# Two buffers for a state space loop's tiles, a cached-row tile in the first stage's memory, and priority for the loop's body

## The chip, the cores and the metric

The kernel runs on one core of a Trainium2 chip. The metric is the time of one execution on the device in microseconds (us); lower is better. The engines are named as the profile names them: PE is TensorE (matmuls and transposes), PEld its weight loads, DVE is VectorE, ACT is ScalarE, POOL is GpSimd and SP is SyncE, which here only issues transfers (DMAs).

## What is computed

One inference step of one layer of a decoder, for a prompt of 512 tokens and for 8 sequences that are decoded one token further. The reference, cut to what matters here:

```python
mod = jnp.dot(jax.nn.silu(c), lp['w_ada']) + lp['b_ada']          # 6 x 1024 shifts, scales, gates
h = modulate(x, lp['norm_attn'], sh1, sc1)
u, q, k_c, v_c, k_s, v_s, k_w, v_w, g = jnp.split(jnp.dot(h, lp['w_in']), offsets, axis=-1)
o_ssm, s_last = ssm_mixer(u, ssm_s0, lp)      # 32 groups of 16 channels, 64 complex states each
o_attn, win_state = attend(q, gates, kv_cmp, kv_slc, kv_win)      # compressed, selected, window branch
x = x + gt1 * jnp.dot(jnp.concatenate([rmsnorm(o_ssm), rmsnorm(o_attn)]), lp['w_out'])
x = x + gt2 * jnp.dot(jnp.square(jax.nn.relu(jnp.dot(h2, lp['w_up']))), lp['w_down'])

def ssm_mixer(u, s0, lp):                     # per group: bu = u @ b_bar; s = lam_bar * s + bu; y = Re(s @ c)
    z = jax.nn.gelu(y + lp['ssm_d'] * u)
    return z * jax.nn.sigmoid(jnp.dot(z, lp['ssm_w_glu'])), s_last

def compress(kv, pe, w1, w2):                 # blocks of 32 cached rows become one row
    h = h_first[:, :-1] + h_second[:, 1:] + jnp.einsum('jd,jdh->h', pe, w1)
    return jnp.einsum('bngh,hd->bngd', jax.nn.gelu(h), w2)
```

`attend` for the 8 sequences compresses 1024 cached rows of each, gathered through a page table.

## The kernel before

The program is one function whose work a scheduler orders: it simulates the engines, and whenever an engine is free it takes the ready instruction that stands highest, which without a priority is the one written first. The order is fixed at build time; on the chip each engine takes its instructions in that order, waits included. Tiles come from pools. A tile with one buffer is written again only after its last reader of the round before; with two buffers, one round may be written while the other is read.

The work around the change, in program order:

- **Cached rows.** `load_cache(b)` gathers the rows of a sequence (POOL). `turned(bp)` transposes two sequences (a pair): 8 groups of four PE transposes `pxc` (L368), each into one of two buffers of the PSUM tag "tr", each taken to the tile `xc` by four copies; for the pairs 2 and 3 all four are ACT's (L375). `compressed(bp)` runs the matmuls `ph` (L387) on the two tiles `xc` of a pair. Of `xc` there are three buffers.
- **Modulation.** `ada(s, tag)` multiplies c by 512 columns of `w_ada`: eight matmuls `pada` (L334), whose weights `wada` (two halves of 1 MB) are loaded through SP's queue (L330) into a raw pool of three buffers; then ACT's copy `mrow` and four transposes `padt`.
- **Keys and values, queries.** `kv_proj` (matmuls `pkv`, L647); the query projection (matmuls `pj`, L605), whose PSUM buffers ACT empties with `ql` and `QS` (L912, L913).
- **The state space loop.** `for qd in range(8)` handles 4 of the 32 groups each, called a quad here. DVE builds the tables `BP` and `Cb` (L752 to L759); PE makes `pm` (L766) and `pbb` (L767); `M` goes to memory as `mscr` (L772) and comes back as the matrix `Tz` (L774), both through SP's queue; ACT copies `Bb` (L769). PE then multiplies the input `U` by `Bb` (`pvs`, L792), ACT copies the result as `Vs` and, with the complex halves turned, `Vp` (L230, L231); DVE forms `W`, scans it into `Rr` (L803), ACT turns that into `Rp`, DVE makes `Sx`, and PE adds `U`,`Tz` (L819) and `Sx`,`Cb` (L820) into `pys`. ACT copies `ys`, SP stores it as `yscr` (L822). The tiles are in the pool `sl`, one buffer each.
- Between quads stand `turned(2)` (ahead of quad 0), `compressed(2)` (quad 2), `turned(3)` (quad 3), `compressed(3)` (quad 5) and five `ada` (quads 1, 3, 4, 6, 7). `U` is loaded by eight transfers on SP's queue (L722) just ahead of quad 0.
- Afterwards `state_space_outputs` takes `yscr` back (`yc`), adds D times u (`yf`, L890) and applies the gelu (`zt`, L108 to L113), beside the query projection and the start of the attention, whose scores are `pst` (L1217) and whose exponentials are `pe` (L1227).

Of the kernel before, what the change touches and what calls it, by code (L numbers as in the profile page):

```python
# [9 lines left out]
F32 = mybir.dt.float32  # L10
# [6 lines left out]
P = 128  # L17
# [19 lines left out]
def body(tc, i, o, dbg=None):  # L37
# [174 lines left out]
    NG = 32  # L212
# [140 lines left out]
    def turned(bp):  # L353
        xc = [cp.tile([P, 2, 8, 132], F32, tag="xc", name="xc", bufs=3) for n in range(2)]
        for n in range(2):
# [229 lines left out]
    for k in range(KT):  # L585
        affine_split(p0, hH[:, k, 0:T], hL[:, k, 0:T], x_tile(k), bc[0], A1[:, k, 0:1], mod[:, k, 0:1])
    p0x.close()
    compressed(1, xcs.pop(1))

# [136 lines left out]
    yscr = dram.tile([NG // GQ, P, GQ, 80], F32, name="yscr")  # L726
    for qd in range(NG // GQ):

        if qd in (0, 3):
            b = 4 + 2 * (qd // 3)  # L730
            load_cache(b)
            load_cache(b + 1)
            xcs[b // 2] = turned(b // 2)
        if qd in (2, 5):
            compressed(2 + qd // 3, xcs.pop(2 + qd // 3))
        if qd in (1, 3, 4, 6, 7):
            ada((5, 6, 7, 8, 9)[(1, 3, 4, 6, 7).index(qd)], "ad")
        if qd == 6:
            compress_prompt()
            dump("Vbd", Vbd)  # L740
        gs = slice(qd * GQ, (qd + 1) * GQ)
# [8 lines left out]
        tmp = sl.tile(b4, F32, tag="tmp", name="tmp")  # L750
        BP = sl.tile(b4, F32, tag="BP", name="BP")
        nc.vector.tensor_tensor(BP, lam_b(lr, 0), vec_b(P1[:, gs]), ALU.mult)  # L752
# [22 lines left out]

        CT = sl.tile([P, GQ, 8, 8], F32, tag="CT", name="CT")
        ST = sl.tile([P, GQ, 8, 8], F32, tag="ST", name="ST")
        tq = sl.tile([P, GQ, 8, 8], F32, tag="tq", name="tq")
# [817 lines left out]
```

## Time and profile before

| | |
|---|---|
| Time, median of 3 runs | 898.34 us (898.29 to 901.24) |
| Profiled execution | 896.29 us, of which the span from first to last instruction is 894.6 us |
| PE busy | 844.3 us (94%), granted clock 0.992 on average |
| PEld, DVE, ACT, POOL busy | 747.3 (84%), 525.0 (59%), 388.2 (43%), 65.2 us (7%) |
| Chain that ended last | PE 86%, DMA 6%, ACT 3%, DVE 2%, issue 1% |

The profile is of one execution. Busy time is that of an engine's instructions; idle time stands in brackets before the instruction that ended it, with the releaser by the trace. The state space loop runs from about 128 to 259 us; the query projection and `state_space_outputs` from 259 to about 300.

### The profile page before, as it was taken

To read this page: it belongs to the slowest core of one execution; us is meant where nothing else is said; L and a number is where in the kernel's file an instruction comes from. 1 tells how busy PE (TensorE), PEld (TensorE's weight loads), DVE (VectorE), ACT (ScalarE), POOL (GpSimd) and SP (SyncE) were. 2 spreads that over 40 slices of the span, in tenths; PEclk is the share of its full clock that TensorE was granted. 3 is DMA by queue.
4 is the path that set the end of the run, shared out by engine and by line. 5 is a ranking of instruction groups with operands and counts; after the bars stand their busy time and mean duration, and the time that the engine had idled before them with its cause. 6 is when DMAs were issued, how large, how long until landed. Compare 5 with 4: busy or idle time off the path is not lost.

```text
span 894.6 us, 16415 instructions
## 1 busy us (share of the span) xinstructions
PE 844.3 (94%) x6517; PEld 747.3 (84%) x6517; DVE 525.0 (59%) x1413; ACT 388.2 (43%) x880; POOL 65.2 (7%) x147
## 2 busy tenths in 40 slices
PE   3799998999999899999889999999999999999995
PEld 2567897788998676756579999999999999999995
DVE  6676656759747975667578964443233444434534
ACT  2545326634435656546655554441111344433422
POOL 6001201000134200100000000000000000000000
PEclk9999999999999999999999999999999999999998
DMA  8956678366456620303257552333333333332202
GB/s 294 318 193 217 194 169 239 123 204 194 127 179 206 203 95 1 142 1 142 78 206 227 161 189 85 95 95 95 95 95 95 95 95 95 96 88 70 79 1 95
DMA packets 111836, 122.36 MB, mean 137 GB/s; under 512 B 24500, under 2 KB 91880, under 8 KB 109584
## 3 DMA queue, kind: packets, MB, share of 16 engines
q1 hardware_dynamic: 102256, 89.71, 33.0%
q0 software_dynamic: 5488, 29.99, 9.8%
q10 hardware_dynamic: 4016, 1.62, 0.7%
q8 instruction: 51, 0.84, 0.4%
q14 instruction: 25, 0.20, 0.1%
HBM read 112.47 MB, written 13.03 MB: 140 GB/s over the span
## 4 chain that ended last, share of the span: by engine, by line
PE 86%; DMA 6%; ACT 3%; DVE 2%; issue 1%; SPq 0%; ACTq 0%; DVEq 0%
PE pdn L1401 21%; PE pup L1401 20%; PE pj L605 5%; PE pwo L1401 5%; PE pkv L647 5%; PE ph L387 5%; DMA wada<-w_ada 5%; PE pada L334 2%; PE ptp L1246 2%; PE po L1253 2%; PE pS L1032 2%; PE pg L1273 2%; PE pst L1217 2%; PE pys L819 2%; PE pkT L1023 1%; PE pst L1218 1%
## 5 line engine op out<-in xcount | busy, mean ns | idle before, releaser
L1401 PE MATMUL pdn<-hidL,wH 128*128 128x256 f32 (+1 forms) x480 | 136.1, 284 | 0.0
L1401 PE MATMUL pdn<-hidH,wL 128*128 128x256 f32 (+1 forms) x480 | 135.9, 283 | 0.0
L1401 PE MATMUL pdn<-hidH,wH 128*128 128x256 f32 (+1 forms) x480 | 135.4, 282 | 0.0
L1401 PE MATMUL pup<-h2L,wH 128*128 128x256 f32 (+1 forms) x480 | 135.0, 282 | 0.0
L1401 PE MATMUL pup<-h2H,wL 128*128 128x256 f32 (+1 forms) x480 | 135.0, 282 | 0.0
L1401 PE MATMUL pup<-h2H,wH 128*128 128x256 f32 (+1 forms) x480 | 134.1, 283 | 0.0
L1401 PEld LDWEIGHTS pup<-h2L,wH 128*128 128x128 f32 x480 | 90.4, 188 | 0.8 <-DVE rs_t L97 0.8
L1401 PEld LDWEIGHTS pdn<-hidH,wL 128*128 128x128 f32 x480 | 90.6, 189 | 0.0
L1401 PEld LDWEIGHTS pdn<-hidL,wH 128*128 128x128 f32 x480 | 90.4, 188 | 0.1
L1401 PEld LDWEIGHTS pup<-h2H,wL 128*128 128x128 f32 x480 | 90.4, 188 | 0.0
L1401 PEld LDWEIGHTS pdn<-hidH,wH 128*128 128x128 f32 x480 | 90.4, 188 | 0.0
L1401 PEld LDWEIGHTS pup<-h2H,wH 128*128 128x128 f32 x480 | 89.6, 188 | 0.0
L63 ACT CAST wH<-wdn 128x1024 fp32r<-128x1024 f32 x30 | 31.5, 1050 | 114.0 <-PE pdn L1401 104.1
L64 DVE TENSOR_TENSOR wL<-wup,wH 128x1024 fp32r<-128x1024 f32 x30 | 36.7, 1224 | 58.1 <-ACT wH L63 58.1
L64 DVE TENSOR_TENSOR wL<-wdn,wH 128x1024 fp32r<-128x1024 f32 x30 | 36.8, 1225 | 54.2 <-ACT wH L63 54.2
L387 PE MATMUL ph<-xc,w 128*128 128x256 f32 (+2 forms) x320 | 65.4, 356 | 1.2 <-DVE xc L377 0.7
L387 PEld LDWEIGHTS ph<-xc,w 128*128 128x128 f32 x320 | 52.8, 203 | 12.9 <-issue 6.4
L63 ACT CAST wH<-wup 128x1024 fp32r<-128x1024 f32 x30 | 31.5, 1050 | 48.0 <-PE pup L1401 37.6
L1479 ACT ACTIVATE rl<-pup 128x256 f32<-128x256 f32 (+1 forms) x64 | 24.4, 384 | 48.9 <-PE pup L1401 48.8
L375 ACT COPY xc<-pxc 64x256 f32<-64x256 f32 x96 | 32.1, 366 | 20.8 <-DVE xc L377 18.2
L1410 DVE SCALAR_TENSOR_TENSOR xT<-pdn,mod,xT 128x256 f32<-128x256 f32 x32 | 15.2, 479 | 43.2 <-PE pdn L1401 43.2
L1480 DVE TENSOR_TENSOR rl<-rl 128x256 f32<-128x256 f32 (+1 forms) x64 | 27.1, 425 | 22.6 <-ACT rl L1479 22.6
(557 smaller groups left out, 2023.9 us busy)
## 6 DMA issues: line engine op xcount, KB each, us to landing
wada<-w_ada SPq DMA_DIRECT2D x20, 1024.0 KB
wup<-w_up SPq DMA_DIRECT2D x16, 1024.0 KB
wdn<-w_down SPq DMA_DIRECT2D x16, 1024.0 KB
wo<-w_out SPq DMA_DIRECT2D x8, 1024.0 KB
wada<-w_ada SPq DMA_DIRECT2D x8, 512.0 KB
rwin<-state_win SPq DMA_DIRECT2D x4, 1024.0 KB
new_win_sample<-state_win POOLq DMA_DIRECT2D x2, 2044.0 KB, 8.9
wkv<-w_in SPq DMA_DIRECT2D x3, 1024.0 KB
```

Of the source, the lines that this page charges most:

```text
L63: nc.scalar.copy(h, src)
L64: nc.vector.tensor_tensor(l, src, h, ALU.subtract)
L334: nc.tensor.matmul(ps[k % 4 * 32 : k % 4 * 32 + 32], cT[:, k], rs[k // kp][:, k % kp], start=(k < 4), stop=(k >= 4))
L375: nc.scalar.copy(dst[:, :, :, hf], srcv[:, :, :, hf])
L387: nc.tensor.matmul(phv[:, lo:hi, 0:w], w1[n][:, r_], xc[n][:, lo:hi, r_ % 8, off : off + w], start=(r_ == 0), stop=(r_ == 15))
L605: nc.tensor.matmul(ps[:, 0:HB], w[:, k], x[:, k, hc], start=(k == 0 and n == 0), stop=(k == KT - 1 and n == 2))
L647: nc.tensor.matmul(ps[0:mp, 0:nw], x[:, k, tok], w[:, k % 4], start=(k == 0 and n == 0), stop=(k == KT - 1 and n == 2))
L819: nc.tensor.matmul(py[:, c], Tz[:, :, :, g].rearrange("p t c -> p (t c)"), U[:, qd * GQ + g], start=True, stop=False)
L1032: nc.tensor.matmul(S[b4 * 32 : b4 * 32 + 32], q4[:, 4 * grp + b4], kts[b4], start=True, stop=True)
L1401: nc.tensor.matmul(ps[:, 0 : b - a], w, x[:, a:b], start=first and n == 0, stop=last and n == 2)
L1479: nc.scalar.activation(rl, ps[:, 0 : b - a], AF.Relu)
L1480: nc.vector.tensor_tensor(rl, rl, rl, ALU.mult)
```

## The change

It gives the tiles `BP`, `CT`, `ST`, `Vs`, `Vp` (shared with `Rp`), `W`, `W2`, `Rr` and `Sx` two buffers. `M`, `Bb`, `Cb`, `Tz`, `tmp`, `tq`, `rho` and `ys` keep theirs. `xc` gets two buffers instead of three; the first `xc` of pair 1 becomes a tile of the pool `p0`, the first stage's memory, and so `compressed(1)` is written ahead of that pool's end. The small tile `so` takes `tmp`'s memory. The quad's body becomes a function that is called under `tc.high_priority(300)`: the scheduler ranks its instructions higher than their place in the program would. No arithmetic is added or taken away.

```diff
     def turned(bp):
-        xc = [cp.tile([P, 2, 8, 132], F32, tag="xc", name="xc", bufs=3) for n in range(2)]
+
+        xc = [p0.tile([P, 2, 8, 132], F32, name="xc1") if (bp, n) == (1, 0) else cp.tile([P, 2, 8, 132], F32, tag="xc", name="xc", bufs=2)
+              for n in range(2)]
...
+    compressed(1, xcs.pop(1))
     p0x.close()
-    compressed(1, xcs.pop(1))
...
-    for qd in range(NG // GQ):
-
-        if qd in (0, 3):
...
+    def quad(qd):
         gs = slice(qd * GQ, (qd + 1) * GQ)
...
-        BP = sl.tile(b4, F32, tag="BP", name="BP")
+        BP = sl.tile(b4, F32, tag="BP", name="BP", bufs=2)
...
-        CT = sl.tile([P, GQ, 8, 8], F32, tag="CT", name="CT")
-        ST = sl.tile([P, GQ, 8, 8], F32, tag="ST", name="ST")
+        CT = sl.tile([P, GQ, 8, 8], F32, tag="CT", name="CT", bufs=2)
+        ST = sl.tile([P, GQ, 8, 8], F32, tag="ST", name="ST", bufs=2)
...
-        Vp = sl.tile([P, GQ, 64], F32, tag="Vp", name="Vp")
+        Vp = sl.tile([P, GQ, 64], F32, tag="Vp", name="Vp", bufs=2)
...
-        Sx = sl.tile([P, GQ, 81], F32, tag="Sx", name="Sx")
+        Sx = sl.tile([P, GQ, 81], F32, tag="Sx", name="Sx", bufs=2)
...
+    for qd in range(NG // GQ):
+
+        if qd in (0, 3):
+            b = 4 + 2 * (qd // 3)
+            load_cache(b)
+            load_cache(b + 1)
+            xcs[b // 2] = turned(b // 2)
+        if qd in (2, 5):
+            compressed(2 + qd // 3, xcs.pop(2 + qd // 3))
+        if qd in (1, 3, 4, 6, 7):
+            ada((5, 6, 7, 8, 9)[(1, 3, 4, 6, 7).index(qd)], "ad")
+        if qd == 6:
+            compress_prompt()
+            dump("Vbd", Vbd)
+        with tc.high_priority(300):
+            quad(qd)
```

(`Vs`, `W`, `W2`, `Rr` and `Rp` change as `Vp` does.) Each engine's instructions up to the end of the key and value projection keep their order but for a few table steps of DVE. Three places move; the line numbers of the changed kernel differ by 2 up to the loop, by 11 less inside it and by 6 more behind it.

PE at the end of `kv_proj(0)`, where the first quad meets pair 2. Before:

```order
L334 MATMUL pada<-wada,cT 32x512 x4
L368 MATMUL pxc<-ident,rc 128x128 x8
L792 MATMUL pvs<-U,Bb 128x72 x4
L368 MATMUL pxc<-ident,rc 128x128 x8
L334 MATMUL pada<-wada,cT 32x512 x4
L368 MATMUL pxc<-ident,rc 128x128 x4
L819 MATMUL pys<-U,Tz 128x80
L766 MATMUL pm_1644<-C_136,BP 128x16 x4
L368 MATMUL pxc<-ident,rc 128x128 x4
L339 MATMUL padt<-ident,mrow 128x128 x4
L767 MATMUL pbb<-ident,BP 128x128 x4
L387 MATMUL ph<-xc,w_155 128x2x128 x4
```

And with the change:

```order
L334 MATMUL pada<-wada,cT 32x512 x4
L781 MATMUL pvs<-U,Bb 128x72 x4
L370 MATMUL pxc<-ident,rc 128x128 x8
L808 MATMUL pys<-U,Tz 128x80
L755 MATMUL pm_1644<-C_136,BP 128x16 x4
L370 MATMUL pxc<-ident,rc 128x128 x4
L756 MATMUL pbb<-ident,BP 128x128 x4
L370 MATMUL pxc<-ident,rc 128x128 x4
L334 MATMUL pada<-wada,cT 32x512 x4
L370 MATMUL pxc<-ident,rc 128x128 x4
L781 MATMUL pvs<-U,Bb 128x72 x4
L809 MATMUL pys<-Sx,Cb 128x80
```

The first quad's `pvs` has moved ahead of all 32 transposes of the pair (12 stood ahead of it, four of them among the `pm` and `pbb` just before the rows shown); the second quad's `pvs` has moved ahead of the last 12. Six more `pys`, 12 transposes and the four `padt` then stand ahead of or among the first `ph`.

ACT at the same place. Before:

```order
L375 COPY xc<-pxc 64x4x64 x4
L769 COPY Bb<-pbb 128x512
L375 COPY xc<-pxc 64x4x64 x8
L793 COPY Vs<-pvs 128x288
L230 COPY Vp<-pvs 64x256
L231 ACTIVATE Vp<-pvs 64x256
L375 COPY xc<-pxc 64x4x64 x8
L230 COPY Rp<-Rr 64x256
L231 ACTIVATE Rp<-Rr 64x256
L336 COPY mrow<-pada 128x512
L375 COPY xc<-pxc 64x4x64 x8
L769 COPY Bb<-pbb 128x512
```

With the change, where the first `Bb` stands further up, among the copies `kvt`:

```order
L782 COPY Vs<-pvs 128x288
L230 COPY Vp<-pvs 64x256
L231 ACTIVATE Vp<-pvs 64x256
L377 COPY xc<-pxc 64x4x64 x8
L230 COPY Rp<-Rr 64x256
L231 ACTIVATE Rp<-Rr 64x256
L377 COPY xc<-pxc 64x4x64 x4
L758 COPY Bb<-pbb 128x512
L377 COPY xc<-pxc 64x4x64 x4
L336 COPY mrow<-pada 128x512
L377 COPY xc<-pxc 64x4x64 x4
L782 COPY Vs<-pvs 128x288
```

The 12 copies `xc` ahead of the first `Vs` are behind it now. Behind the rows shown come `Vp` twice, `ys` and nine copies `xc`. On SP's queue `wada`, which stood between `mscr` and `Tz` of quad 0, now stands behind that `Tz`.

ACT in the query projection, where `state_space_outputs` runs beside it. Before:

```order
L63 CAST wH<-wq 128x1024
L912 ACTIVATE ql<-pj 64x260
L913 ACTIVATE QS<-pj 64x252
L912 ACTIVATE ql<-pj 64x260
L913 ACTIVATE QS<-pj 64x252
L108 ACTIVATE zt<-yf 128x520
L111 ACTIVATE zt<-zt 128x520
L63 CAST wH<-wq 128x1024
L912 ACTIVATE ql<-pj 64x260
L913 ACTIVATE QS<-pj 64x260
```

With the change:

```order
L919 ACTIVATE QS<-pj 64x260
L63 CAST wH<-wq 128x1024
L111 ACTIVATE zt<-zt 128x520
L918 ACTIVATE ql<-pj 64x260
L919 ACTIVATE QS<-pj 64x252
L918 ACTIVATE ql<-pj 64x260
L919 ACTIVATE QS<-pj 64x252
L918 ACTIVATE ql<-pj 64x260
L919 ACTIVATE QS<-pj 64x260
```

The gelu's steps `zt` and the cast `wH` no longer both stand between two rounds of `QS`: the next cast `wH` comes after the `QS` that frees the PSUM buffer.

## Rows read from the trace of the kernel before

**Rows 1.** The page: busy time, share of the span and instructions of each engine; the chain that ended last, by engine.

```profile
PE 844.3 (94%) x6517; PEld 747.3 (84%) x6517; DVE 525.0 (59%) x1413; ACT 388.2 (43%) x880; POOL 65.2 (7%) x147
...
PE 86%; DMA 6%; ACT 3%; DVE 2%; issue 1%; SPq 0%; ACTq 0%; DVEq 0%
```

**Rows 2.** Busy time by stretch: the stretch and its length, then PE, PEld, DVE, ACT and POOL busy us (with instructions), the granted clock of PE, the DMA share and GB/s.

```profile
130.00:140.00 10.00, 8.54 (x76) 6.71 (x76) 7.11 (x23) 5.51 (x16) 0.00 (x0) 1.00 1.17 183
140.00:150.00 10.00, 8.93 (x60) 7.09 (x59) 6.67 (x19) 9.02 (x27) 2.99 (x5) 1.00 0.88 269
...
170.00:180.00 10.00, 8.82 (x62) 6.81 (x61) 8.25 (x21) 9.74 (x29) 0.89 (x3) 1.00 0.88 289
180.00:280.00 100.00, 99.94 (x747) 89.79 (x744) 69.86 (x182) 40.78 (x105) 20.21 (x49) 1.00 0.60 185
280.00:300.00 20.00, 18.66 (x123) 14.37 (x123) 16.33 (x38) 11.51 (x31) 8.11 (x21) 1.00 0.53 150
300.00:320.00 20.00, 16.75 (x104) 11.59 (x106) 16.57 (x63) 12.17 (x37) 1.48 (x6) 1.00 0.43 148
```

**Rows 3.** PE's timeline in the two stretches in which the loop meets a pair of cached rows: start, duration, line, operation, tiles, shape, count, and the idle time before it with its releaser. A matmul of the order above shows as two instructions here, a transpose as one.

```profile
134.96 1.07 PE L334 MATMUL pada<-wada,cT 128*32 128x512 f32 x8
135.96 1.09 PE L368 MATMUL pxc<-ident,rc 128*128 128x128 f32 x8
138.51 1.08 PE L792 MATMUL pvs<-U,Bb 128*128 128x72 f32 x8 [1.46 <-DMA new_cmp_sample<-kvs]
139.43 1.04 PE L368 MATMUL pxc<-ident,rc 128*128 128x128 f32 x8
141.53 1.07 PE L334 MATMUL pada<-wada,cT 128*32 128x512 f32 x8 [1.07 <-DMA wada<-w_ada]
...
143.45 1.00 PE L766 MATMUL pm<-C,BP 128*128 128x16 f32 x8
...
150.28 0.34 PE L820 MATMUL pys<-Sx,Cb 128*128 128x80 f32 x2
...
152.52 1.05 PE L792 MATMUL pvs<-U,Bb 128*128 128x72 f32 x8
...
173.86 1.06 PE L766 MATMUL pm<-C,BP 128*128 128x16 f32 x8 [0.55 <-ACT Vp L231]
...
178.23 1.99 PE L387 MATMUL ph<-xc,w 128*128 128x256 f32 x8 [0.52 <-ACT xc L375]
```

**Rows 4.** ACT's timeline in the first of these stretches, in the same columns.

```profile
134.73 1.29 ACT L375 COPY xc<-pxc 64x256 f32<-64x256 f32 x4 [0.88 <-PE pxc L368]
136.04 0.59 ACT L769 COPY Bb<-pbb 128x512 f32<-128x512 f32 x1
136.65 2.59 ACT L375 COPY xc<-pxc 64x256 f32<-64x256 f32 x8
139.63 0.40 ACT L793 COPY Vs<-pvs 128x288 f32<-128x288 f32 x1 [0.39 <-PE pvs L792]
...
140.43 0.38 ACT L231 ACTIVATE Vp<-pvs 64x256 f32<-64x256 f32 x1
...
143.74 0.41 ACT L231 ACTIVATE Rp<-Rr 64x256 f32<-64x256 f32 x1
...
152.72 0.43 ACT L821 COPY ys<-pys 128x320 f32<-128x320 f32 x1 [3.12 <-PE pys L820]
```

**Rows 5.** SP's queue: when transfers were issued and how long the issuing took; and behind it one piece of the chain that ended last (start, us, what), the time from issue to landing of `wada`.

```profile
127.00 5.11 SPq L722 DMA_DIRECT2D U<-uscr  x8
135.38 0.34 SPq L772 DMA_DIRECT2D mscr<-M  x1
...
138.62 0.37 SPq L774 DMA_DIRECT2D Tz<-mscr  x1
...
136.09 5.41 DMA wada<-w_ada
```

**Rows 6.** What DVE waited for between 125 and 260 us: engine, tile, line, releaser, then us in total, times and the longest.

```profile
DVE Cb L757 <- PE pys L820: 15.2, 5, 5.3
```

**Rows 7.** The query projection: PE's timeline, then ACT's.

```profile
281.34 0.39 PE L605 MATMUL pj<-hH,wH 128*128 128x260 f32 x1 [1.40 <-ACT QS L913]
...
278.12 0.64 ACT L111 ACTIVATE zt<-zt 128x520 f32<-128x520 f32 x1 [2.03 <-DVE zt L110]
278.88 1.04 ACT L63 CAST wH<-wq 128x1024 fp32r<-128x1024 f32 x1
...
280.92 0.37 ACT L913 ACTIVATE QS<-pj 64x260 fp32r<-64x260 f32 x1
```

**Rows 8.** The start of the attention: PE's timeline, then ACT's, then DVE's.

```profile
312.40 0.33 PE L1217 MATMUL pst<-KH,QS 128*128 128x128 f32 x1 [1.14 <-ACT pe L1227]
...
305.76 0.64 ACT L111 ACTIVATE zt<-zt 128x520 f32<-128x520 f32 x1
...
310.16 0.69 DVE L113 TENSOR_TENSOR uT<-zt,yf 128x520 f32<-128x520 f32 x1
```

**Rows 9.** Busy time by stretch, in the columns of rows 2, at places where PE stood idle for long.

```profile
14.00:18.00 4.00, 0.99 (x5) 0.62 (x4) 3.73 (x25) 1.47 (x4) 1.75 (x3) 1.00 1.07 312
...
36.00:40.00 4.00, 1.88 (x10) 0.85 (x10) 3.14 (x9) 2.71 (x9) 0.00 (x0) 1.00 1.02 392
40.00:44.00 4.00, 3.66 (x14) 2.00 (x15) 0.00 (x0) 0.00 (x0) 0.00 (x0) 0.57 1.04 386
```

More of the change, by code (lines that the diff above doesn't have):

```diff
@@ L726, in body @@
     yscr = dram.tile([NG // GQ, P, GQ, 80], F32, name="yscr")
-    for qd in range(NG // GQ):
-        if qd in (0, 3):
[L730 to L740, printed above, removed]
+    def quad(qd):
         gs = slice(qd * GQ, (qd + 1) * GQ)
@@ L786, in body @@
         nc.gpsimd.memset(rho[:, :, 0:1], 0.0)
-        Vs = sl.tile([P, GQ, 72], F32, tag="Vs", name="Vs")
+        Vs = sl.tile([P, GQ, 72], F32, tag="Vs", name="Vs", bufs=2)
         pvv = pst("ss", "pvs")
@@ L794, in body @@
         nc.vector.tensor_tensor(sn[:, :, gs], sn[:, :, gs], Vs[:, :, 64:72].rearrange("p g b -> p b g"), ALU.add)
-        Vp = sl.tile([P, GQ, 64], F32, tag="Vp", name="Vp")
+        Vp = sl.tile([P, GQ, 64], F32, tag="Vp", name="Vp", bufs=2)
         turn(Vp, pvv[:, 0 : GQ * 72].rearrange("p (g c) -> p g c", g=GQ)[:, :, 0:64])
-        W = sl.tile([P, GQ, 64], F32, tag="W", name="W")
-        W2 = sl.tile([P, GQ, 64], F32, tag="W2", name="W2")
+        W = sl.tile([P, GQ, 64], F32, tag="W", name="W", bufs=2)
+        W2 = sl.tile([P, GQ, 64], F32, tag="W2", name="W2", bufs=2)
         nc.vector.tensor_tensor(W, Vs[:, :, 0:64], CT, ALU.mult)
@@ L801, in body @@
         nc.vector.tensor_tensor(W, W, W2, ALU.add)
-        Rr = sl.tile([P, GQ, 64], F32, tag="Rr", name="Rr")
+        Rr = sl.tile([P, GQ, 64], F32, tag="Rr", name="Rr", bufs=2)
         nc.vector.tensor_tensor_scan(Rr.rearrange("p g c -> p (g c)"), rho.rearrange("p g c -> p (g c)"),
                                      W.rearrange("p g c -> p (g c)"), 0.0, ALU.mult, ALU.add)
-        Rp = sl.tile([P, GQ, 64], F32, tag="Vp", name="Rp")
+        Rp = sl.tile([P, GQ, 64], F32, tag="Vp", name="Rp", bufs=2)
         turn(Rp, Rr)
-        Sx = sl.tile([P, GQ, 81], F32, tag="Sx", name="Sx")
+        Sx = sl.tile([P, GQ, 81], F32, tag="Sx", name="Sx", bufs=2)
         nc.gpsimd.memset(Sx[:, :, 0:1], 0.0)
@@ L827, in body @@
     nc.tensor.transpose(px[0:NG, 256:384], SF, ident)
-    so = sl.tile([P, 384], F32, name="so")
+    so = sl.tile([P, 384], F32, tag="tmp", name="so")
     nc.vector.tensor_copy(so[:, 0:256], px[:, 0:256])
```

## Prediction

> **What bounds the kernel now.** I read the page first: PE is busy 94% of the span and holds 86% of the chain that ended last, ACT 3% and DVE 2% [rows 1]. No arithmetic changes, so the time can only move by PE's idle time, 894.6 - 844.3 = 50.3 us over the whole span. The second view is busy time by stretch, which says where that idle time lies. In the loop's first 50 us it is 1.46 us (130 to 140), 1.07 (140 to 150) and 1.18 (170 to 180), 3.71 together; from 180 to 280 us it is 0.06 us in 100 [rows 2]. So six of the eight quads already run beside a full PE. Right behind the loop it is 1.34 us (280 to 300) and 3.25 (300 to 320) [rows 2]. The rest lies at the start, from 320 us on and at the end, where the order changes little; I cost that at nothing, with about 1.5 us either way.
>
> The third view is PE's timeline at the two places, with the releaser of each wait [rows 3]. The first `pvs` waited 1.46 us for a transfer until 138.51. The transfer named is the tiny store of `kvs`; I take it for `U`, which `pvs` reads and whose last load was issued by 132.1 [rows 5]: nothing else that `pvs` needs is late, `Bb` being done at 136.63 [rows 4]. `pada` waited 1.07 us for `wada`, which took 5.41 us from issue to landing [rows 3, 5]. In the second place PE waited 0.55 and 0.52 us for ACT [rows 3], which was busy 9.74 of those 10 us [rows 2]: with all copies of a pair on it, ACT is the bound there. No wait repeats from quad to quad on PE. The one that does is DVE's: five times, 15.2 us together, `Cb` waits for the last `pys` of the quad before [rows 6]. That is the wait of a tile with one buffer, but `Cb` keeps one.
>
> One page of the notes bears on this. The Trainium skill, Perfetto Trace Analysis, section Optimization Strategy, says that a gap that keeps repeating on the engine that should be saturated can mean too few buffers. By that rule, read against the rows above, the second buffers are worth nothing on PE, at most the 0.06 us of 180 to 280; the repeating gap is on an engine that is not the bound, and its tile isn't doubled. By DVE's row alone one might hope for a share of 15.2 us.
>
> **Part by part.** *Buffers.* They remove waits of DVE, ACT and POOL, under a PE with 0.06 us idle: 0. That cover is gone only where PE waits already, at the two pairs and behind the loop, and there the order decides. *The tile `xc1` in the first stage's memory, and `so`.* PE's order up to the end of `kv_proj(0)` is as before; 0. *Priority.* It moves the quad's instructions past the transposes and copies of the pairs. I walked the new order with the durations of before.
>
> *First pair, PE.* Four transposes that stood ahead of `pada` take 0.5 us (eight took from 135.96 to 137.05); without them `pada` ends at about 135.5 instead of 135.96 [rows 3]. Behind it stands `pvs`, and `U` is there at 138.5: 3.0 us idle. Before, eight transposes (135.96 to 137.05) filled a part of it. Then:
> - `pvs` takes 0.9 us (138.51 to 139.43), eight transposes 1.0: 140.4. ACT, whose copies now can't start before `Vs`, does `Vs` and twice `Vp` until 140.8 [rows 4], then the first group of four copies, 1.29 us [rows 4], until 142.1. A `pys` and `pm` (0.1 and 1.0) end at 141.5, and the third group of transposes waits for a PSUM buffer: 0.6 us idle.
> - The third group and `pbb` (0.5 each) end at 143.1; the second group's copies at 143.4: 0.3 idle. The fourth group and `pada` (1.0) end at 144.9.
> - ACT does `Rp` twice (0.8), then the third group until 145.5: 0.6 idle before the fifth group. `Bb` of quad 1 (0.59) ends at 146.1, the fifth group at 146.0: 0.1 idle, then `pvs` until 147.0.
> - Seven `pys` (2.0, eight took from 150.28 to 152.52 [rows 3]), the sixth group, `padt` and the seventh (0.5 each) end at 150.5. ACT after `Bb`: the fourth group 147.4, `mrow` 148.0, the fifth group 149.3, `Vs`, twice `Vp` and `ys` 150.9, and `ph` needs three copies of the sixth group (in the row of 178.23 it started at the third copy's end), 151.9: 1.4 idle.
>
> Sum 3.0 + 0.6 + 0.3 + 0.6 + 0.1 + 1.4 = 6.0 us, where before it was 2.53 (1.46 + 1.07): **+3.5**. In it `wada`'s wait is 0: it now stands behind `Tz`, which was issued at 138.62; with 5.41 us it lands at 144.0 [rows 5], as `pada` is reached. The reason for the loss in one line: ACT did 12 copies, 3.9 us (1.29 + 2.59), while the first `pvs` waited for `U` [rows 4]. Now it waits too, and does them later.
>
> *Second pair.* The same walk with the quads 2 and 3, where no transfer is late, gives waits of 0.4, 0.8 and 0.3 = 1.5 us for 1.18: **+0.3**. Its bounds are 0 idle (-1.2), if the quads' earlier chains give ACT a lead, and 6.0 idle (+4.8), as in the first pair.
>
> *The query projection.* `pj` waited 1.40 us for `QS` [rows 7]. Ahead of those copies ACT had waited 2.03 us for DVE in the gelu, then did `zt` and the cast `wH` [rows 7]. In the new order `QS` of the next half stands ahead of the cast. Gain between 0 (another DVE wait in front of `QS`) and 1.4; I take **-1.0**, nearer the full one, since the cast's 1.04 us alone comes off the path.
>
> *Start of the attention.* The last quad's `pys` come some 6.7 us of PE's work earlier in the order, so the four rounds of `yf` and `zt` do too, by about 4 us; ACT's `zt` (0.64) and DVE's last step at 310.16 no longer stand between the softmax steps that PE waited for (1.14 us on `pe`) [rows 8]. Of the 3.25 us idle in 300 to 320 [rows 2] the gelu's instructions on ACT and DVE are about half of what was ahead of the waits; bounds 0 and -3.25, taken **-1.5**.
>
> Sum: 3.5 + 0.3 - 1.0 - 1.5 = +1.3 us. Against the profiled execution, 896.29, that is 897.6; the median of the runs is 2.05 higher, 898.34, which makes 899.6.
>
> **Rivals.** A measurement of this kernel can tell about 0.5%, 4.5 us: faster means below 893.85, slower above 902.83.
> - *Faster: the earlier quads win everywhere.* The first pair costs only `U` (+1.5) and saves `wada` (-1.07), because ACT catches up under `ph`; the second pair's 1.18, the 1.40 of `pj` and the 3.25 go: 898.34 + 0.4 - 5.8 = 892.9. For it: DVE's and ACT's chains do start earlier in the order. Against: PE has no other ready work at the first pair, as `ph` needs the very copies. Chance 0.2.
> - *Slower: ACT's queue bounds both pairs.* If the second pair costs what the first does (6.0 idle), the time is 899.6 + 4.5 = 904.1. ACT had 0.26 us to spare in 170 to 180 [rows 2], and each quad puts seven of its own copies, 3.0 us, ahead of the pair's. It decides from 4.7 us idle at the second pair on. Chance 0.2.
> - *The clock falls.* After 36 to 40 us, with PE busy 1.88 of 4 us, the granted clock was 0.57 for 4 us, which costs 4 x 0.43 = 1.7 us; after the 3.01 us of waiting in 14 to 18 us it stayed at 1.00 [rows 9]. If the idle time at 135.5 brings it down: 901.3. The Trainium skill, TensorE: Matmul & The Clock Gate, section Why this matters for your kernels, advises against long idle gaps between bursts of matmuls, which speaks for this rival; by that rule, too, it would be about 901. The rows show both outcomes. Chance 0.1.
> - *Nothing moves.* Loss and gains are hidden, the idle time at both pairs stays 3.7 us: 898.3. For it: 0.06 us in 100. Against: the first `pvs` has nothing to stand behind. Chance 0.1.
>
> **How the numbers follow.** The forecast itself has 0.4, within 896 to 903 by the bounds of its four terms taken singly. The time is 899.6. The range goes from the faster rival's 892.9 to the slower one's 904.1, with 0.6 of spread at either end: 892.5 to 904.7. Faster by over 0.5%: the faster rival less its upper edge, 0.18; slower: the slower rival and a little of the clock's, 0.22; the same 0.6.
>
> **What would show it.** Right: before the first `pvs` a wait of 3 us, and PE waiting at `pxc` and `ph` for ACT's copies between 140 and 153; no wait of `pada` for `wada`; the loop's idle time 7 to 8 us; less than 0.7 at `pj`; less than 2.5 in the 20 us after the projection. Wrong: a `pvs` that starts well before 138, which would say that not `U` was late; an ACT that is idle in the second pair; or a change of more than 2 us behind 320 us, which I set to nothing.

## The result, and the profile after

The change made the kernel slower: 908.93 us median of four executions (904.89 to 911.93), where the kernel before, run beside it, took 898.32 (895.51 to 901.24). The ratio is 1.0129, with a 95% interval of 1.0082 to 1.0175. The forecast was 899.6, in a range up to 904.7. The profiled execution of the change took 911.73 us, its span is 910.0 us, and the mean granted clock in it 0.985 (0.992 before).

The page of the profiled execution, busy time of each engine and the chain that ended last, to be held against [rows 1]:

```profile
PE 853.8 (94%) x6517; PEld 752.3 (83%) x6517; DVE 527.1 (58%) x1413; ACT 389.0 (43%) x880; POOL 64.6 (7%) x147
...
PE 80%; DMA 9%; DVE 5%; ACT 3%; issue 1%; SPq 0%; POOL 0%; DVEq 0%; ACTq 0%
```

The first thing to see is PE's busy time: 853.8 us where it was 844.3, with the same 6517 matmuls. 9.5 of the 15.4 us by which the span grew are not waits at all. So the ground of the prediction, that time can only move by PE's idle time, is gone before any wait is read.

Two things make the same matmuls longer: a lower clock, and an order in which they go less well together. To part them we used landmarks. The same matmuls lie ahead of the first `pj` (a projection ahead of the loop), the last `pj`, the last `po` that reads `PT` (the end of the attention), the first `pup` and the last `pup` in both kernels. So their start times can be subtracted. From each difference we take the time that the low clock cost: half of every stretch at the lower of PE's two levels, 1.2 instead of 2.4 GHz. What remains is waits and longer work. (In a stretch in which PE also waits, half of it is too much.)

| start of | before | after | difference | low clock | rest | rest since the landmark above |
|---|---|---|---|---|---|---|
| first `pj` | 93.1 | 93.6 | +0.5 | 0 | +0.5 | +0.5 |
| last `pj` | 295.2 | 305.6 | +10.4 | 5.1 | +5.3 | +4.8 (the loop) |
| last `po` | 448.9 | 459.9 | +11.1 | 5.1 | +6.0 | +0.7 (attention) |
| first `pup` | 503.5 | 515.9 | +12.5 | 5.1 | +7.4 | +1.4 (out-projection) |
| last `pup` | 786.6 | 802.1 | +15.4 | 6.8 | +8.6 | +1.3 (MLP) |

Of the 15.4 us the clock holds 6.8, the loop 4.8, the passage from the out-projection to the MLP 2.7, the rest 1.2. The loop's 4.8 can be parted once more: between its landmarks PE's idle time grew by 2.2 us (7.3 for 5.1) and its busy time by 7.7, of which the clock holds 5.1. So 2.2 us are waits and 2.6 us are longer work.

**The first pair.** Busy time by stretch, in the columns of [rows 2]; the third and fourth lines cut out the idle time and what came behind it:

```profile
130.00:140.00 10.00, 6.88 (x60) 5.16 (x59) 7.44 (x26) 1.22 (x3) 0.00 (x0) 0.97 1.00 111
140.00:150.00 10.00, 8.53 (x59) 6.96 (x58) 6.39 (x17) 8.73 (x25) 2.68 (x5) 0.86 0.68 210
136.00:139.00 3.00, 0.09 (x4) 0.00 (x0) 1.66 (x10) 0.00 (x0) 0.00 (x0) 1.00 0.89 104
139.00:143.00 4.00, 3.79 (x20) 3.83 (x21) 1.30 (x4) 1.93 (x6) 0.00 (x0) 0.57 0.75 206
```

PE's timeline there, as [rows 3], then ACT's, as [rows 4]:

```profile
135.03 1.06 PE L334 MATMUL pada<-wada,cT 128*32 128x512 f32 x8
139.21 1.71 PE L781 MATMUL pvs<-U,Bb 128*128 128x72 f32 x8 [3.12 <-DMA new_cmp_sample<-kvs]
140.70 1.92 PE L370 MATMUL pxc<-ident,rc 128*128 128x128 f32 x8
...
146.48 1.07 PE L334 MATMUL pada<-wada,cT 128*32 128x512 f32 x8 [0.97 <-DMA wada<-w_ada]
...
149.48 0.45 PE L809 MATMUL pys<-Sx,Cb 128*128 128x80 f32 x2 [0.50 <-POOL Sx L802]
...
153.54 1.99 PE L389 MATMUL ph<-xc,w 128*128 128x256 f32 x8 [0.24 <-ACT xc L377]
```

```profile
141.00 0.40 ACT L782 COPY Vs<-pvs 128x288 f32<-128x288 f32 x1 [5.73 <-PE pvs L781]
```

And `wada` in the chain that ended last, from issue to landing, as in [rows 5]:

```profile
139.46 6.98 DMA wada<-w_ada
```

This is the walk of the prediction: `pada` first, then nothing for `pvs` to stand behind, 3.12 us of waiting, and an ACT that does nothing for 5.73 us. The waits of the stretch are 3.12 + 0.97 + 0.50 + 0.24 = 4.83 us for 2.53 before. Behind the idle 3 us the clock fell to 0.57 of full in the four microseconds from 139, which costs 4 x 0.43 = 1.7 us.

**Inside the quads.** PE's timeline behind the second pair, of the change and then of before:

```profile
178.29 0.66 PE L370 MATMUL pxc<-ident,rc 128*128 128x128 f32 x4 [0.41 <-ACT xc L377]
179.60 0.66 PE L370 MATMUL pxc<-ident,rc 128*128 128x128 f32 x4 [0.66 <-ACT xc L377]
...
183.32 1.05 PE L334 MATMUL pada<-wada,cT 128*32 128x512 f32 x2
184.29 0.66 PE L400 MATMUL pk<-w2v,hg 128*128 128x64 f32 x4
...
185.33 1.06 PE L334 MATMUL pada<-wada,cT 128*32 128x512 f32 x6
186.32 0.66 PE L370 MATMUL pxc<-ident,rc 128*128 128x128 f32 x4
...
197.82 1.06 PE L334 MATMUL pada<-wada,cT 128*32 128x512 f32 x6
198.81 1.11 PE L781 MATMUL pvs<-U,Bb 128*128 128x72 f32 x8
199.85 1.91 PE L334 MATMUL pada<-wada,cT 128*32 128x512 f32 x10
201.68 0.48 PE L389 MATMUL ph<-xc,w 128*128 128x256 f32 x1
```

```profile
186.80 1.92 PE L334 MATMUL pada<-wada,cT 128*32 128x512 f32 x16
188.65 0.70 PE L387 MATMUL ph<-xc,w 128*128 128x256 f32 x2
```

The first two lines are the second pair's waits: 1.07 us, as before (0.55 + 0.52 [rows 3]). The `pada` lines are what nobody had looked for. A `pada` matmul writes 32 of the 128 output partitions, four of them stand in the order one behind the other, and PE runs the four side by side: eight instructions of the trace (four matmuls) take 1.00 us (135.03 to the next start, [rows 3] has the same), sixteen take 1.85 (186.80 to 188.65). Now the priority draws a quad's matmuls forward, through the middle of such a set. Two instructions alone then take 0.97 us (183.32 to 184.29), the six that were cut off from them 0.99 (185.33 to 186.32): nearly two full prices for one set. In the same way six and ten, cut by a `pvs`, take 0.99 + 1.83 where sixteen whole ones take 1.85. The order has three such cuts, each some 0.97 us dearer: **2.9 us of PE work** that the kernel before doesn't have. The same price shows, with the other sign, in the matmuls `psc` of the attention, which have the same shape (128x32): between the first and the last `pj` the change has them in one piece fewer, and they take 1.0 us less.

**Between out-projection and MLP.** PE's timeline, of the change and then of before; `bc` is the broadcast of the MLP norm's statistics, from which `h2H` and `h2L`, the operands of `pup`, are made:

```profile
513.11 0.29 PE L1407 MATMUL pwo<-mixH,wqL 128*128 128x264 f32 x1
513.23 0.61 PE L1378 MATMUL bc<-dg,ones 128*128 128x128 f32 x4
515.94 0.50 PE L1407 MATMUL pup<-h2H,wH 128*128 128x256 f32 x2 [2.10 <-ACT h2H L200]
...
517.40 0.39 PE L1407 MATMUL pup<-h2L,wH 128*128 128x256 f32 x1 [0.72 <-DVE h2L L201]
```

```profile
499.86 0.38 PE L1372 MATMUL bc<-dg,ones 128*128 128x128 f32 x2
...
503.35 0.29 PE L1401 MATMUL pwo<-mixH,wqL 128*128 128x264 f32 x1
503.47 0.40 PE L1401 MATMUL pup<-h2H,wH 128*128 128x256 f32 x2
```

Before, `bc` stood ahead of the last 26 `pwo`, and the norm's 2 to 3 us on ACT and DVE ran beside them; `pup` began without a wait. Now `bc` is PE's last instruction before `pup`, and the norm has nothing beside it: 2.10 + 0.72 us. This lies some 250 us behind the last quad.

**The clock.** Busy time by stretch at the two places, besides 139 to 143, where it was low in this profile and not in that of before:

```profile
224.00:232.00 8.00, 8.00 (x38) 5.30 (x37) 5.57 (x16) 3.24 (x6) 0.37 (x2) 0.57 0.05 8
...
514.00:518.00 4.00, 1.34 (x9) 1.14 (x10) 4.00 (x11) 1.69 (x4) 0.00 (x0) 1.00 0.24 85
518.00:522.00 4.00, 4.00 (x28) 3.98 (x30) 3.89 (x10) 2.39 (x5) 0.00 (x0) 0.57 0.81 265
```

The fall at 518 stands behind the idle time at `pup`. That at 224 doesn't: PE was busy 8.00 of 8 us. Three places, 4 + 8 + 4 us at 0.57, make 1.7 + 3.4 + 1.7 = 6.8 us. This profile lost more than the others: in the runs of experiment e4, by each execution's span and mean clock, four executions of the change lost 11.3 us to the clock on average and seven of before 8.3, a difference of 3.0; without it 894.1 us stand against 886.7, **+7.4**.

**The rest of the loop and the attention**, in the columns of [rows 2], and the query projection as in [rows 7]:

```profile
170.00:180.00 10.00, 8.94 (x64) 6.71 (x63) 6.91 (x20) 6.53 (x20) 1.04 (x4) 1.00 0.29 95
180.00:280.00 100.00, 99.17 (x683) 84.97 (x682) 61.14 (x165) 40.32 (x107) 14.58 (x42) 0.97 0.58 183
290.00:310.00 20.00, 19.01 (x137) 15.48 (x135) 15.79 (x36) 11.79 (x29) 7.99 (x21) 1.00 0.44 114
310.00:330.00 20.00, 17.49 (x88) 10.69 (x88) 16.95 (x64) 11.35 (x34) 1.68 (x6) 1.00 0.52 183
...
295.82 0.39 PE L607 MATMUL pj<-hH,wH 128*128 128x260 f32 x1 [0.58 <-ACT QS L919]
```

PE is still full from 180 to 280 (99.17 of 100), so the second buffers have nothing to give there, but the same work is longer. `pj` waits 0.58 for 1.40. In the 20 us around the start of the attention PE is idle 2.51 us for 3.25, yet by the landmarks the attention as a whole gained nothing (+0.7): over all of it PE waits only 0.1 us less, and its matmuls `pS`, again four side by side, stand in one piece more and take 1.1 us longer.

### The profile page after: what moved, and what is told of

Its sections match the earlier page's. It is cut to its first block, busy times and chain, and to the rows that moved or that the text cites. A ratio compares the mean times of both kernels' runs of the same rounds, so it can differ in the third digit from the quotient of the medians.

```text
span 910.0 us, 16408 instructions
## 1 busy us (share of the span) xinstructions
PE 853.8 (94%) x6517; PEld 752.3 (83%) x6517; DVE 527.1 (58%) x1413; ACT 389.0 (43%) x880; POOL 64.6 (7%) x147
## 4 chain that ended last, share of the span: by engine, by line
PE 80%; DMA 9%; DVE 5%; ACT 3%; issue 1%; SPq 0%; POOL 0%; DVEq 0%; ACTq 0%
PE pup L1407 20%; PE pdn L1407 20%; PE pwo L1407 5%; DMA wada<-w_ada 5%; PE ph L389 4%; PE pkv L649 3%; PE pada L334 3%; PE pj L607 3%; PE ptp L1252 2%; PE po L1259 2%; PE pg L1279 2%; PE pS L1038 2%; PE pys L808 1%; DMA yc<-yscr 1%; PE pst L1223 1%
## 5 line engine op out<-in xcount | busy, mean ns | idle before, releaser
L334 PE MATMUL pada<-wada,cT 128*32 128x512 f32 x192 | 34.2, 635 | 6.0 <-DMA wada<-w_ada 5.3
```

The costliest lines, as they stand in the source:

```text
L334: nc.tensor.matmul(ps[k % 4 * 32 : k % 4 * 32 + 32], cT[:, k], rs[k // kp][:, k % kp], start=(k < 4), stop=(k >= 4))
```

## Experiments

Each run is compared with the kernel before on the same chip. The table has what the edits below came to: the ratio with its interval; the rest against before, stretch by stretch, as in the table of landmarks; what the low clock cost in the loop and in the attention; the `pada` sets that are cut in the loop, and how much longer `pada` takes there; how many `pwo` stand behind `bc`; how many of PE's 1039 instructions in the attention stand elsewhere than before, by matching the orders of the two traces; and the whole rest once more, over all executions.

| run | median | ratio | rest: loop, attention, out-proj., MLP | clock: loop, att. | cuts, `pada` | `pwo` behind `bc` | moved in att. | rest, all executions |
|---|---|---|---|---|---|---|---|---|
| the change | 908.93 | 1.0129 [1.0082, 1.0175] | +4.8 +0.7 +1.4 +1.3 | 5.1, 0 | 3, +2.9 | 0 | 102 | as e4 |
| e4, again | 907.33 | 1.0126 [1.0100, 1.0152] | +3.3 +0.4 +1.4 +1.4 | 3.4, 0 | 3, +3.0 | 0 | 102 | +7.4 |
| e1 | 918.30 | 1.0236 [1.0182, 1.0290] | -2.5 +3.4 +2.5 +0.9 | 1.7, 17.1 | 0, 0 | 0 | 602 | +8.9 |
| e2 | 912.59 | 1.0171 [1.0121, 1.0221] | -4.0 +4.0 +0.9 0 | 3.4, 10.2 | 1, +1.0 | 26 | 663 | +3.5 |
| e3 | 905.65 | 1.0109 [1.0081, 1.0137] | +4.1 -0.5 0 0 | 5.1, 1.7 | 3, +2.8 | 26 | 87 | +5.4 |
| e5 | 903.82 | 1.0064 [1.0034, 1.0095] | +0.2 0 +2.3 +1.4 | 3.4, 0 | 0, 0 | 0 | 92 | +3.7 |
| e6 | 905.50 | 1.0092 [1.0063, 1.0122] | +5.5 -0.2 0 0 | 6.8, 1.7 | 4, +3.9 | 26 | 87 | +6.1 |
| e7 | 909.91 | 1.0125 [1.0085, 1.0165] | +5.6 -0.1 +1.7 +1.1 | 5.1, 0 | 5, +4.8 | 0 | 87 | +8.5 |
| e8 | 910.83 | 1.0131 [1.0088, 1.0174] | +5.6 -0.1 +2.3 +1.4 | 3.4, 1.7 | 3, +2.9 | 0 | 95 | +8.6 |
| e9 | 899.98 | 1.0027 [0.9994, 1.0060] | +0.1 -0.2 0 0 | 6.8, 1.7 | 0, +0.1 | 26 | 92 | +2.6 |
| e10 | 907.54 | 1.0107 [1.0082, 1.0131] | +0.4 -0.9 +2.3 +1.2 | 0, 6.8 | 0, 0 | 0 | 653 | +3.8 |
| e11 | 903.99 | 1.0069 [1.0028, 1.0111] | +2.9 -0.7 +1.7 +0.5 | 1.7, 1.7 | 0, +0.2 | 0 | 87 | +4.7 |

The rest and the clock stretch by stretch come from one profiled execution each, so single entries scatter by a microsecond or more (e4 is the change once more, and its loop shows +3.3 for +4.8); what lies ahead of the first `pj` (-3.6 to +1.6) isn't in them. Two columns are steadier. `pada` is PE's time from the start of each `pada` instruction to PE's next start, summed between the first and the last `pj`, low clock at half: it follows the number of cuts at 0.95 to 1.01 us each, and is within 0.2 us of before where nothing is cut. The last column takes each execution's span, less what its mean clock says was lost, on average, against the same for the kernel before.

**e1: the priority taken away**, all buffers as in the change.

```diff
-        with tc.high_priority(300):
-            quad(qd)
+        quad(qd)
```

> The change with the priority taken away; second buffers, the tile in the first stage's memory and the earlier compressed(1) stay. In its order the first pvs again stands behind 12 transposes of the pair, as before, but the broadcast bc of the MLP's norm stands behind the last pwo, as with the change (before, 26 pwo stood behind it). Theory P (the priority costs the wait of 3.1 us at the first pvs and the fall of the clock behind it): that wait is 1.4 to 1.6 us again and the clock stays up there. Theory L (the wait of 2.8 us ahead of pup, and the fall behind it, come from where bc stands, not from the priority): still 2 to 3 us of waiting ahead of pup; together 900 to 903 us. Rival B (the second buffers and the moved tile cost the time in the loop): the loop stays 5 us longer, 905 to 909. Rival of L (the priority makes the late wait): 898.

Measured 918.3 us, the slowest of all, though the loop is 2.5 us better than before: the first `pvs` waits 0.80 us. The loss lies where the edit does nothing: in the attention, of whose 773 matmuls 525 stand elsewhere by the built order. PE waits there 8.1 us more than before (18.1 for 10.0, from the last `pj` to the last `po`), and the clock is charged 17.1 us, which is too much where PE also waits, and `pS`, in fewer pieces here, takes 2.3 us less; hence a rest of only +3.4. The windows of it show stretches of 20 us at 0.83 to 0.86, one of them with PE busy 19.11 of 20:

```profile
297.00:317.00 20.00, 15.41 (x73) 8.82 (x71) 17.13 (x51) 10.90 (x31) 5.59 (x14) 0.86 0.67 227
417.00:437.00 20.00, 19.11 (x95) 11.68 (x94) 12.60 (x34) 10.05 (x30) 0.00 (x0) 0.83 0.04 17
437.00:457.00 20.00, 16.70 (x150) 11.84 (x151) 12.47 (x40) 12.18 (x34) 0.96 (x1) 0.83 0.73 253
```

So without any priority the buffers and the tile `xc1` together change the order far behind the tiles that they are about.

**e2: the priority for all quads but the first.**

```diff
-        with tc.high_priority(300):
+        with tc.high_priority(300 if qd else 0):
```

> The change, with the priority for quads 1 to 7 but not for quad 0. In its order the first pvs stands behind 12 transposes and bc ahead of 26 pwo, both as before. P and L: wait at the first pvs 1.4 to 1.6, ahead of pup under 0.6, no fall of the clock at 139 or 518 us; 896 to 899 us. Rival B: 901 or more, since the buffers are all there.

Measured 912.59 us. `pvs` waits 1.08 us and the loop is 4.0 us better than before, with one cut set in it: PE's idle time there is 2.6 us under that of before, so what the first quad's priority costs at the first pair comes back, and more. The attention, dealt out anew as in e1, has 6.3 us more of waits, a rest of +4.0 and 10.2 by the clock.

**e3: the priority alone**, on the buffers of before.

```diff
+    def quad(qd):          # the body of the loop, tiles as before
...
+        with tc.high_priority(300):
+            quad(qd)
```

> The kernel before with the priority alone: one buffer each, three for xc, compressed(1) at its old place. In its order 4 transposes stand ahead of the first pvs (12 before, none with the change) and bc stands ahead of 26 pwo. P: wait at the first pvs about 2.6 us, perhaps with the fall of the clock; ahead of pup under 0.6; 899 to 902 us. Rival B: 898, no loss without the buffers.

Measured 905.65 us: the loop's loss is the priority's (+4.1, `pvs` waits 2.99 us, three cuts), and with this order `bc` stands where it was and nothing is lost behind the loop but 1.7 us by the clock.

**e4: the change once more**, run beside e1 to e3; no edit.

> The change itself once more, for the clock of each execution. If the falls of the clock at 225 to 232 and at 518 us belong to the kernel, every run loses 12 us or more to a lowered clock, 909 to 912 us. If they come and go from run to run, some runs show a mean clock of 0.990 or more, at about 904, and others 0.985 or less, at about 911; the waits (8.6 us more than before up to the last pup) are in both.

Measured 907.33 us; its four executions lie between 904.54 and 909.39, at mean clocks of 0.990 to 0.985.

**e5: buffers without priority, and `CT` and `ST` back to one.**

```diff
-        CT = sl.tile([P, GQ, 8, 8], F32, tag="CT", name="CT", bufs=2)
-        ST = sl.tile([P, GQ, 8, 8], F32, tag="ST", name="ST", bufs=2)
+        CT = sl.tile([P, GQ, 8, 8], F32, tag="CT", name="CT")
+        ST = sl.tile([P, GQ, 8, 8], F32, tag="ST", name="ST")
...
-        with tc.high_priority(300):
-            quad(qd)
+        quad(qd)
```

> As e1 (no priority), and CT and ST have one buffer again; the other seven tiles keep two. Its order is that of before in the loop (3 matmuls of 1101 elsewhere) and nearly so in the attention (68 of 773; in e1 525), but bc stands behind the last pwo, as with the change and in e1. Theory A (e1 and e2 lost their time where the scheduler dealt the attention out anew: more waits there, and a clock that falls because PE is less densely used): about 902 us, that is before plus 2.6 us of waits and a fall of the clock at the start of pup; no fall between 300 and 440 us. Rival B (the second buffers themselves): 910 or more, as e1.

Measured 903.82 us. Only three matmuls of the loop move, and it takes what it took before: +0.2 us. Seven second buffers bring nothing. All of its loss behind the loop is `bc`, which stands behind the last `pwo` here too, with the same waits as in the change:

```profile
506.20 0.61 PE L1377 MATMUL bc<-dg,ones 128*128 128x128 f32 x4
508.90 0.50 PE L1406 MATMUL pup<-h2H,wH 128*128 128x256 f32 x2 [2.10 <-ACT h2H L200]
```

**e6: the change with one buffer for `CT` and `ST`.** The edit is the first half of e5's.

> The change with its priority, but CT and ST with one buffer. In its order the first pvs stands ahead of all transposes as with the change, the attention is as before (64 elsewhere), and bc stands ahead of 26 pwo, as before. Theory L: the wait ahead of pup is under 0.6 us and the clock stays up there; waits 2.6 us fewer than with the change from the last po to the last pup; 903 to 905 us. Rival of L (the late wait comes with the loop's priority): as the change, 907 to 909.

Measured 905.5 us: `pvs` (3.25 us) as in the change, a fourth cut, `bc` back ahead of 26 `pwo`, and nothing lost behind the loop but 1.7 us by the clock. Here a second buffer of two tiles of the loop moves an instruction that runs some 380 us behind the loop's start. It isn't those two tiles alone that decide it: e8 has one buffer for them too, and there `bc` stands behind the last `pwo`.

**e7: a priority of 100 instead of 300.**

```diff
-        with tc.high_priority(300):
+        with tc.high_priority(100):
```

> The change with a priority of 100 instead of 300: 8 transposes stand ahead of the first pvs (none with the change, 12 before), 32 ahead of the second (20, 32); attention nearly as before, bc behind the last pwo. Theory P: half of the loop's loss, wait at the first pvs 1.9 to 2.2 us, waits of the loop between before (29.2 us by the same count) and the change (34.0): about 31; 903 to 906 us. Rival (the first pair is not where the loop loses): as the change in the loop, 907 to 909.

Measured 909.91 us. Now eight `pxc` stand ahead of the first `pvs`, which waits 1.28 us instead of 3.12. The loop as a whole got nothing back (+5.6): PE's idle time there is only 0.7 us over that of before, where the change has 2.2, but the sets are cut into more pieces (1, 3, 4; 1, 6, 1; 1, 7; 3, 5 matmuls), and `pada` takes 4.8 us more instead of 2.9. What the waits gave, the cuts took.

**e8: the first quad's `pvs` doesn't read `U`.** It multiplies by the identity, so the first quad's state and outputs are left out; `CT` and `ST` have one buffer.

```diff
-            nc.tensor.matmul(..., Bb[:, g], U[:, qd * GQ + g, 0:72], ...)
+            nc.tensor.matmul(..., Bb[:, g], U[:, qd * GQ + g, 0:72] if qd else ident[:, 0:72], ...)
```

> As e6, and the first quad's pvs reads the identity instead of U (so quad 0's state and outputs are left out of the computation): pvs no longer needs U's loads. bc stands behind the last pwo. If U is what the first pvs waits for (the trace names the store of kvs): the wait of 3.1 us ahead of it goes, under 0.6 us is left, and the clock does not fall there; the loop is 3 us shorter in its waits than with the change. If it is the store or its copy kvs: the wait stays.

Measured 910.83 us. PE's timeline:

```profile
134.77 1.00 PE L781 MATMUL pvs<-ident,Bb 128*128 128x72 f32 x8
...
142.25 0.73 PE L808 MATMUL pys<-U,Tz 128*128 128x80 f32 x2 [4.45 <-DMA Tz<-mscr]
```

`pvs` starts without a wait, so it was `U` that it waited for. But the `pys` behind it reads `Tz`, whose transfer the priority hasn't made earlier, and PE waits 4.45 us for that: the wait went one step on. Behind the first wait stood a second, which here costs more.

**e9: the change, with the five `pada` sets of the loop kept whole** by a higher priority of their own.

```diff
-        for k in range(KT):
-            nc.tensor.matmul(ps[k % 4 * 32 : k % 4 * 32 + 32], cT[:, k], ...)
+        with tc.high_priority(600 if 5 <= s < 10 else 0):
+            for k in range(KT):
+                nc.tensor.matmul(ps[k % 4 * 32 : k % 4 * 32 + 32], cT[:, k], ...)
```

> The change, and the matmuls pada of the five ada in the loop rank higher still (600), so that no quad's matmul comes between the eight of a set. With the change three sets are cut (by the order 1+3, 3+5, 5+3 matmuls of the rows); the trace shows 0.98 us for a piece of one matmul, 0.99 for one of three and 1.00 for a whole four. In the order of this kernel no set is cut, the first pvs still stands ahead of all transposes, the attention is as before (68 of 773 elsewhere) and bc ahead of 26 pwo. Theory C (cut sets cost 2.9 us of the loop): the waits and cuts of the loop fall from 34.0 us by our count to 31, near 29.2 of before plus the 2.3 of the first pair; with bc in its place the whole is 5.5 us below the change in its waits: 899 to 902 us. Rival (the hidden 2.9 us are waits for buffers): 34 in the loop, 903 to 905.

Measured 899.98 us, a time that these runs can't tell from before. PE's timeline:

```profile
137.66 1.08 PE L782 MATMUL pvs<-U,Bb 128*128 128x72 f32 x8 [2.98 <-DMA U<-uscr]
...
197.52 1.92 PE L335 MATMUL pada<-wada,cT 128*32 128x512 f32 x16
```

The wait for `U` is as long as in the change, and the profile names it here. The sixteen instructions that were cut in six and ten stand together again, `pada` takes what it took before (+0.1), and the loop's rest goes from +4.8 to +0.1. That looks too good: PE's idle time in the loop is 1.4 us over that of before, and in this profile PE waited 0.8 us inside a stretch of 10.2 us at the low clock that is charged with half its length. Over all executions e9 stands 2.6 us above before, about what the first pair costs (+2.3 in the change). `bc` came back ahead of 26 `pwo` as well, which gives the other 2.7 us; the two gains lie in different stretches, so they can be told apart. e3 and e11 have one of the two each: three cuts with `bc` in its place stand at +5.4, no cut with `bc` behind the last `pwo` at +4.7.

**e10: the cached-row tile alone**: `xc1` in the first stage's memory, `compressed(1)` a step earlier; one buffer for the quad's tiles, no priority.

```diff
-        BP = sl.tile(b4, F32, tag="BP", name="BP", bufs=2)
+        BP = sl.tile(b4, F32, tag="BP", name="BP")      # and so for the eight others
...
-        with tc.high_priority(300):
-            quad(qd)
+        quad(qd)
```

> The kernel before with nothing of the change but the tile xc1 in the first stage's memory, two buffers for xc and compressed(1) a line earlier; no second buffers in the loop, no priority. In its order the loop is as before (24 of 1101 elsewhere, no cut sets), but the attention is dealt out anew (483 of 773 elsewhere) and bc stands behind the last pwo. Theory A (the attention's new order loses the time of e1 and e2, by waits and a falling clock): 908 to 918 us, with falls of the clock between 300 and 470 us. Rival (it was the second buffers of CT and ST): 899 to 902.

Measured 907.54 us. The loop is unharmed (+0.4). The attention has 483 matmuls moved by the built order; PE waits there 3.6 us more than before, and 6.8 us are charged to the clock, in stretches like this one (PE was busy 19.50 of these 20 us before, at 1.00):

```profile
380.00:400.00 20.00, 18.16 (x122) 10.52 (x120) 11.38 (x40) 9.04 (x21) 0.00 (x0) 0.83 0.00 1
```

The rest there is -0.9 all the same, since its work is shorter (`pS` alone by 1.6 us) and the charge for the clock too high where PE waits. `bc` behind the last `pwo` cost 3.5 us.

**e11: all `pada` sets of the program whole**, the same edit with a priority of 400 everywhere.

> As e9 with a rank of 400 and for all ada of the kernel: no set of the loop is cut, the attention is as before (64), but bc stands behind the last pwo, as with the change. Theory C alone: loop about 31 by our count; from the last po to the last pup 12.6 us of waits as with the change; 903 to 906 us. Rival: as the change, 907 to 909.

Measured 903.99 us. No set of the loop is cut, and `pada` takes what it took before (+0.2). The loop's +2.9 is waits for the most part: the first landmark comes 3.6 us earlier, with the same matmuls ahead of it, and PE's idle time behind it is 2.1 us more than before (`pvs` waits 2.85 us for 1.46, and a `pada` at 94.20 us waits 1.20 for `wada`). By the last `pj` 0.7 us are gained. `bc` stands behind the last `pwo`, and the passage to the MLP loses 2.2 us.

## Why the prediction was wrong

By waits and work the change costs +8.6 us in its profile (+7.4 over the four executions of e4), where the sum said +1.3; the rest is the clock.

- **"The time can only move by PE's idle time" failed**, and with it the largest part. PE's work isn't constant under a new order: three cut `pada` sets are +2.9 us with no wait in any view. The table shows it: `pada`'s time in the loop follows the cuts from run to run at 0.95 to 1.01 us each, from none to five. Where no set is cut the loop's rest is +0.4 or less (e1, e5, e9, e10; e11's +2.9 is mostly waits), with three to five cuts it is +3.3 to +5.6, and e9's edit is on these sets alone, though it moves `bc` too. The new order had the pieces in plain sight, but only the places with waits had been walked.
- **"From 320 us on, nothing" failed**: +2.7 us at `bc`, out of the 1.5 allowed. In the eight profiles with no `pwo` behind `bc` the two last stretches lose 2.2 to 3.7 us together; with 26 behind it 0 (e3, e6, e9), once 0.9 (e2). The prediction said what would refute it, a change of more than 2 us behind 320 us, and this was it.
- **First pair, +3.5: the mechanism held, the size was off**, +2.3 (4.83 for 2.53). `pvs` waits 3.12 us (3.0 in the sum), for `U` as reasoned (e8, e9). But `wada`'s wait, set to 0, is 0.97: behind `Tz` it was issued at 139.46 and took 6.98 us, not 5.41; and ACT's copies, which were to cost 0.6 + 0.3 + 0.6 + 0.1 + 1.4 at five places, cost 0.24 at one and a wait for `Sx` 0.50 at another. Part of this may be the low clock, at which PE needs longer while ACT doesn't. e8 says that the term is no lever by itself: take the wait away, and another stands behind it. In e7 the waits did shrink, but the cuts grew.
- **Second pair, +0.3**: 1.07 us of waits for 1.07, so 0. The rival that ACT bounds both pairs fell: ACT is busy 6.53 of 10 us from 170 to 180.
- **`pj`, -1.0**: -0.82 (0.58 for 1.40), right in size. But it isn't the priority's own gain: `pj` waits 1.40 us as before in eight of the runs (e3 and e5 to e11), with the priority in six of them, and doesn't wait in e1, which has none.
- **Start of the attention, -1.5: nothing.** PE's idle time in the 20 us after the projection is 0.74 less, but over the whole attention only 0.1 us: what was saved at the softmax came back behind it, and `pS`, cut once more, takes 1.1 us longer. That makes the rest of +0.7.
- **Buffers, 0**: right for the loop. e5, with seven second buffers, stands at +0.2. The Trainium skill (Perfetto Trace Analysis, Optimization Strategy) takes a repeating gap on the engine that should be saturated as a possible sign of too few buffers. The trace agrees: PE had no repeating gap, and nothing was gained on PE. "PE's order up to the end of `kv_proj(0)` is as before; 0" holds too for `xc1` (e10, +0.4), but only up to there: the same edit, with one `xc` buffer less, moved 483 matmuls of the attention.
- **The clock**, a rival with 1.7 us and a chance of 0.1, was worth 3.0 us on average over the executions and 6.8 in the profile. It fell at three places instead of one.

The other terms of the profile's +8.6 are small: +0.5 ahead of the loop, +0.6 of waits at the key projections that did not stand there before (0.38 and 0.23).

Two things stay open. Part of e9's +0.1 in the loop, for 1.4 us more of waits, is a clock charged too high, as said there; the rest of that difference we did not find. And why the clock falls so often in the rearranged attention of e1, e2 and e10 none of these runs tells. PE waits more there (18.1, 16.4 and 13.6 us for 10.0 before): in e10 it waited 0.92 us until 389.75 and 0.85 us until 391.47, which it didn't before, and the granted clock was 0.54 from 391 to 395. But it stayed at 1.00 from 407 to 411, where PE waited 2.27 us, and in the change it fell at 224 us without any wait.

## What to carry to other kernels

A priority or one more buffer does not act on its own stage alone: where the order is dealt out by a scheduler, it deals again to the end of the program, and what it moves there can be worth more than what was meant. So compare the new order to its last row, on the engine that bounds the kernel, and look there for two things: sets of small matmuls that run side by side and are now cut, and instructions that begin a chain of other engines (like `bc`) and have lost the work behind which that chain was hidden. When a priority is raised, raise that of such sets with it: in e9 this took the change from 1.3% slower to a time that can't be told from before, though in part because it happened to move `bc` back.

## What was not expected of the hardware

- The price of a set of matmuls that run side by side is paid for each piece of it: 1.00 us for four whole, 0.97 for one and 0.99 for the other three. Another tile's matmul between them is enough, and each cut added 0.95 to 1.01 us in the loop, in seven profiles with one to five cuts.
- The granted clock fell to 0.57 of full from 224 to 232 us with PE busy 8.00 of 8 us, and to 0.83 over 20 us with PE busy 19.11 (e1); a look at PE's idle time alone would not find these. It stayed at 1.00 from 514 to 518, with PE busy 1.34 of 4, and fell only in the stretch behind.
- The executions of one kernel differ in their granted clock: the change took 904.89 us at a mean clock of 0.992 and 911.93 at 0.982.
